# Four edits in the expert layer: x's scale and shift in 16 pieces, a sum's operand in PSUM, finer yields in the index work, fewer transposes on TensorE

## The chip, the cores and the metric

One core of one Trainium2 chip runs the whole kernel. The metric is the time of one execution in device microseconds (us), lower is better. The kernel before was run three times: 2249.8 us median, 2248.74 to 2251.46.

## What is computed

Two layers, each a mixer (two kinds of attention) and then an expert layer (`peer_ffn`), over 256 tokens of width 1024. All four edits lie in the expert layer:

```python
s1 = einsum('bshd,hnd->bshn', q[..., 0, :], sub_keys[0]);  s2 = ...      # 8 heads, 128 keys each
v1, i1 = top_k(s1, 16);  v2, i2 = top_k(s2, 16)
cand = (v1[..., :, None] + v2[..., None, :]).reshape(B, S, PEER_HEADS, 256)
cand_idx = (i1[..., :, None] * 128 + i2[..., None, :]).reshape(...)
top, pos = top_k(cand, 16)
idx = take_along_axis(cand_idx, pos, axis=-1)
gates = softmax(top, axis=-1)
act = gelu(einsum('btd,bthkd->bthk', hb, peer_u[ib]))
out = einsum('bthk,bthkd->btd', gb * act, peer_v[ib])
x = layer_norm(DN_ALPHA * x + out * gt2, ln_g[l, 1], ln_b[l, 1])
```

`layer_norm` ends in a scale by `ln_g` and a shift by `ln_b`. That of the mixer's norm is the one that the first edit cuts into pieces.

## The kernel before

The expert layer doesn't gather. It multiplies all 16384 experts with all tokens: 128 tiles j of `peer_u` (128 experts by 1024), in what is called the U stage here, then 128 tiles of `peer_v` (the V stage). The gates are a matrix of experts by tokens that is zero where an expert wasn't chosen. Every fp32 weight is split into a high half `wh` (ACT copies it to fp32r) and a low half `wl` (weight minus `wh`), and each product is three matmuls: hi x hi, lo x hi, hi x lo. A U tile is 24 matmuls with 256 columns, a V tile 12 with 512.

**Supply of a tile.** `take` hands out a tile that `prep` has split; `fetch` issues the DMA of a tile five ahead on SP's queue (5 buffers `raw`); `turn` transposes a `u` tile one or two ahead on DVE (`STREAM_TRANSPOSE`, L220, in blocks of 32x32, for which the DMA has arranged the rows). Of every four U tiles the fourth is of kind `x`: its DMA lays the rows out plainly, and `prep` (L246 to L251) transposes it on TensorE with eight 128x128 transposes into two PSUM banks, out of which ACT copies `wh` and then the weight itself (L263, L264). In the U stage POOL makes both `wl` of a tile (L271). In the V stage DVE makes them, with the low half of the gated activations (L521) before them.

**Side work.** While TensorE multiplies U tiles, the generators in `sides` make the gates. After each tile `pull` (L635) lets them go on until a credit is used up: 1.55 after a `u` tile, 2.75 after an `x` tile, and each `yield` gives the cost of what came before it. So the written order of DVE's instructions, its transposes among them, follows from these numbers. `select` is first `topk`: for 16 units (8 heads, 2 halves of the tokens) `key_ops` finds 16 best keys in each half, and zipped with it `cand_ops` of the unit before adds the candidates (L1400) and finds the best 16. TensorE's scores for a unit are issued one unit ahead (`scores`, L1371), and ACT copies them out of PSUM. Then the *index work* (L1443 to L1489) turns positions into expert numbers for each half of the tokens: small operations, then for either key a compare, a multiply and a reduce over 128x2048 (L1465, L1468, L1470). Then `place_gates`: 64 groups of 4 tokens, each two DVE operations, eight fp16 matmuls into a PSUM tile `G`, and their copies. The last two U tiles (126 and 127; `U_FIRST`) are multiplied after `sides` is drained.

**Scale and shift of x.** In the V stage, at j = 32, POOL issues the loads of `ln_g` and `ln_b` into rows of a free buffer, and at j = 38 and 44 multiplies and adds them to the two halves of x (L1726 to L1728).

## Time and profile before

| | before |
|---|---|
| runs | 2249.8 us median (2248.74 to 2251.46) |
| profiled execution | 2254.38 us, its span 2252.6 us |
| busy: PE, DVE, ACT, POOL | 95%, 81%, 52%, 46% |
| mean granted clock of TensorE | 0.982 |
| chain that ended last, by engine | PE 73%, DVE 16%, DMA 4%, ACT 3%, issue 3%, POOL 1% |
| chain, by line: U tiles, V tiles, transposes of `x` tiles | 28%, 27%, 2% |

How to read it: times are us from the span's start. The profiled execution is one run; its span is the time from its first to its last instruction. "Busy" is the time in which an engine had an instruction under way, waits inside it included. The chain of work is followed back from the last instruction, at each step to what released it. In the rows below an engine's idle time before an instruction stands in brackets, with what ended it.

### The profile page before, as it was taken

To read this page: it belongs to the slowest core of one execution; us is meant where nothing else is said; L and a number is where in the kernel's file an instruction comes from. 1 tells how busy PE (TensorE), PEld (TensorE's weight loads), DVE (VectorE), ACT (ScalarE), POOL (GpSimd) and SP (SyncE) were. 2 spreads that over 40 slices of the span, in tenths; PEclk is the share of its full clock that TensorE was granted. 3 is DMA by queue.
4 is the path that set the end of the run, shared out by engine and by line. 5 is a ranking of instruction groups with operands and counts; after the bars stand their busy time and mean duration, and the time that the engine had idled before them with its cause. 6 is when DMAs were issued, how large, how long until landed. Compare 5 with 4: busy or idle time off the path is not lost.

```text
span 2252.6 us, 42211 instructions
## 1 busy us (share of the span) xinstructions
PE 2135.2 (95%) x14596; PEld 1945.4 (86%) x14596; DVE 1817.2 (81%) x3278; ACT 1172.5 (52%) x2445; POOL 1041.5 (46%) x760
## 2 busy tenths in 40 slices
PE   5789899899999999999989998998999999999998
PEld 5789799899999978888779897997999999788886
DVE  7887989999997488888887558999999955666675
ACT  3446555455555545555545564554555555455562
POOL 4656637787778510000045534577777783200001
PEclk8999999999999999999999999999999999999999
DMA  8646567666667678888844335675766676666662
GB/s 273 196 137 221 159 140 159 129 148 148 142 147 156 176 236 275 281 286 283 298 134 150 113 121 142 147 153 118 154 142 148 146 164 187 202 196 192 193 227 90
DMA packets 498895, 400.32 MB, mean 178 GB/s; under 512 B 291920, under 2 KB 446072, under 8 KB 498680
## 3 DMA queue, kind: packets, MB, share of 16 engines
q1 hardware_dynamic: 496936, 392.33, 62.8%
q0 software_dynamic: 1408, 4.23, 0.6%
q8 instruction: 115, 1.88, 0.3%
q10 hardware_dynamic: 336, 1.06, 0.1%
q14 instruction: 100, 0.82, 0.1%
HBM read 396.46 MB, written 1.05 MB: 176 GB/s over the span
## 4 chain that ended last, share of the span: by engine, by line
PE 73%; DVE 16%; DMA 4%; issue 3%; ACT 3%; POOL 1%; SPq 1%; POOLq 0%; ACTq 0%; DVEq 0%
PE A L61 28%; PE Y L61 27%; PE T L61 7%; PE G L61 4%; PE T L251 2%; DVE wl L271 2%; PE ss L61 2%; PE hs L61 2%; DMA raw<-in_peer_u_dram 2%; POOL wl L271 1%; DVE qk L857 1%; DMA raw<-in_peer_v_dram 1%; DVE raw L220 1%; DVE e L843 1%; DVE o L1504 1%
## 5 line engine op out<-in xcount | busy, mean ns | idle before, releaser
L271 POOL TENSOR_TENSOR wl<-raw,wh 128x512 fp32r<-128x512 f32 x663 | 914.3, 1406 | 700.9 <-ACT wh L58 582.4
L58 ACT ACTIVATE wh<-raw 128x512 fp32r<-128x512 f32 x1060 | 610.8, 623 | 182.0 <-PE A L61 47.6
L61 PE MATMUL A<-hTh,wh 128*128 128x256 f32 x2080 | 543.3, 293 | 11.9 <-ACT wh L58 11.8
L61 PE MATMUL A<-hTl,wh 128*128 128x256 f32 x2080 | 524.2, 284 | 0.0
L61 PE MATMUL Y<-wh,o 128*128 128x512 f32 x1776 | 480.5, 392 | 0.8 <-DVE o L521 0.8
L271 DVE TENSOR_TENSOR wl<-raw,wh 128x512 fp32r<-128x512 f32 x525 | 380.2, 765 | 63.5 <-ACT wh L58 44.9
L61 PEld LDWEIGHTS A<-hTh,wh 128*128 128x128 f32 x2080 | 400.6, 193 | 14.4 <-ACT wh L58 13.7
L61 PEld LDWEIGHTS A<-hTl,wh 128*128 128x128 f32 x2080 | 401.7, 193 | 0.8 <-DVE hTl L521 0.2
L61 PEld LDWEIGHTS Y<-wh,o 128*128 128x128 f32 x1776 | 334.9, 189 | 70.8 <-DVE o L521 1.2
L61 PE MATMUL A<-hTh,wl 128*128 128x256 f32 x2080 | 337.9, 285 | 11.0 <-POOL wl L271 10.9
L61 PEld LDWEIGHTS A<-hTh,wl 128*128 128x128 f32 x2080 | 288.9, 193 | 14.2 <-POOL wl L271 14.2
L61 PE MATMUL Y<-wl,o 128*128 128x512 f32 x888 | 277.9, 393 | 10.4 <-DVE wl L271 10.4
L220 DVE STREAM_TRANSPOSE raw<-raw 128x1024 f32<-128x1024 f32 x192 | 235.1, 1230 | 11.7 <-DMA raw<-in_peer_u_dram 10.1
L58 ACT ACTIVATE o<-buf 128x256 fp32r<-128x256 f32 x228 | 95.1, 417 | 282.7 <-PE Y L61 282.7
L521 DVE TENSOR_TENSOR o<-buf,o 128x256 fp32r<-128x256 f32 x228 | 100.1, 439 | 150.4 <-ACT o L58 150.4
L61 PEld LDWEIGHTS Y<-wl,o 128*128 128x128 f32 x888 | 168.1, 189 | 48.9 <-DVE wl L271 13.8
L1499 DVE TENSOR_TENSOR o<-iT,iota_t 128x1024 f16<-128x1024 f16 x128 | 163.9, 1280 | 0.0
L58 ACT ACTIVATE buf<-G 128x128 f32<-128x128 f32 (+4 forms) x244 | 56.0, 276 | 203.6 <-PE G L61 203.6
L570 POOL TENSOR_TENSOR x<-x,buf 128x1024 f32<-128x1024 f32 x1 | 2.4, 2392 | 291.0 <-DVE x L567 291.0
L61 PE MATMUL T<-hTh,wh 128*128 128x256 f32 x512 | 133.6, 293 | 0.0
L61 PE MATMUL T<-hTl,wh 128*128 128x256 f32 x512 | 130.1, 286 | 0.0
L1504 DVE TENSOR_TENSOR o<-gT,o 128x1024 f16<-128x1024 f16 x128 | 124.6, 973 | 4.4
(496 smaller groups left out, 3254.9 us busy)
## 6 DMA issues: line engine op xcount, KB each, us to landing
raw<-in_peer_u_dram SPq DMA_DIRECT2D x1024, 128.0 KB, 3.5
raw<-in_peer_v_dram SPq DMA_DIRECT2D x256, 512.0 KB, 4.4
raw<-in_w_in_dram SPq DMA_DIRECT2D x88, 512.0 KB, 4.9
raw<-in_w_ada_dram SPq DMA_DIRECT2D x78, 512.0 KB, 4.9
raw<-in_w_o_dram SPq DMA_DIRECT2D x16, 512.0 KB, 3.5
raw<-in_w_pq_dram SPq DMA_DIRECT2D x64, 128.0 KB, 3.4
qk<-in_w_ada_dram SPq DMA_DIRECT2D x10, 512.0 KB, 3.9
e<-in_w_ada_dram SPq DMA_DIRECT2D x8, 512.0 KB, 6.0
```

The costliest lines, as they stand in the source:

```text
L58: nc.scalar.activation(o, i, f, **kw)
L61: nc.tensor.matmul(o, a, b, start=start, stop=stop, **kw)
L220: nc.vector.transpose(t, t)
L251: nc.tensor.transpose(banks[s][:, q], t[:, (4 * s + q) * P:(4 * s + q + 1) * P], ident)
L271: eng.tensor_sub(lo, src, h.bitcast(F32))
L521: nc.vector.tensor_sub(lo, src, h.bitcast(F32))
L570: nc.gpsimd.tensor_mul(xt[tt], xt[tt], last[0])
L843: eng.tensor_sub(ev[:, :, :hn], mid, bv[:, :, :hn])
L857: nc.vector.tensor_mul(tv[:, :, hn:], nodes(qT, n)[:, :, hn:], ev[:, :, hn:])
L1499: nc.vector.tensor_tensor(o.rearrange("p a u n v -> p (a u) n v"), iT[:, b].rearrange("p a (u v) -> p (a u) v", v=2)[:, :, None] .to_broad ...
L1504: nc.vector.tensor_mul(og.rearrange("p u a n v -> p (u a) n v"), gT[:, b * nu:(b + 1) * nu].rearrange("p u a v -> p (u a) v")[:, :, None] ...
```

## The change

Four edits, all but the first in `peer`:

1. `uv_seq`: tiles 103, 107, ..., 127 (seven in each layer) are of kind `u`, no longer `x`.
2. `topk`: a PSUM tile `vp` is added. Before the two candidate sums of a unit ACT copies the 16 values of the first key list into it (128x16), a yield of cost 0 follows, and both sums read that operand from PSUM.
3. Index work: yields after each of the first operations, and higher costs for the compare (1.4 to 1.7) and the reduce (1.4 to 1.6). What it charges in all goes from 0.9 + 7.8 to 4.2 + 8.8 for each half of the tokens.
4. x's scale and shift: 16 instructions on 256 columns, one after each of the V tiles 38 to 53, in place of four on 1024 columns.

```diff
-    uv_seq = [("x" if j % 4 == 3 else "u", j) for j in range(NK)] + [("v", j) for j in range(NK)]
+    uv_seq = [("x" if j % 4 == 3 and j < 100 else "u", j) for j in range(NK)] + [("v", j) for j in range(NK)]
@@ topk
+                    vp = psk.tile([P, 2, PH, TOPK], F32, name="G")
+
@@ cand_ops
                         at = 0
+                        act(vp[:, tt, h], v[0][tt][:, h], AF.Copy)
+                        yield 0.0
                         for a0, a1, w in segs:
                             dims = [P, a1 - a0, w]
                             nc.vector.tensor_add(cd[:, at:at + dims[1] * w].rearrange("p (a b) -> p a b", b=w),
-                                                 v[0][tt][:, h, a0:a1, None].to_broadcast(dims),
+                                                 vp[:, tt, h, a0:a1, None].to_broadcast(dims),
                                                  v[1][tt][:, h, None, :w].to_broadcast(dims))
@@ index work
                             nc.vector.tensor_scalar(sel[a].bitcast(U32), puf, 4 - 2 * a, None,
                                                     op0=OP.logical_shift_right)
+                            yield 0.5
                             nc.vector.tensor_copy(half[2 + a], iu[a][tt].rearrange("p h k -> p (h k)").bitcast(U32))
+                            yield 0.6
 
                         nc.vector.scalar_tensor_tensor(half[0], sel[1].bitcast(U32), -12.0, sel[0].bitcast(U32),
                                                        op0=OP.add, op1=OP.max)
+                        yield 0.5
                         for a in range(2):
                             nc.vector.scalar_tensor_tensor(sel[a], half[0], -16.0 + 12 * a, puf, op0=OP.mult, op1=OP.add)
+                            yield 0.5
                         nc.vector.scalar_tensor_tensor(half[1], sel[1], -48.0, sel[0], op0=OP.add, op1=OP.max)
                         tp = top[tt]
-                        yield 0.9
+                        yield 0.5
                         for a in range(2):
                             nc.vector.tensor_tensor(m, per_head(half[a])[:, :, :, None].to_broadcast(k4),
                                                     iota_k[:, None, None].to_broadcast(k4), op=OP.is_equal)
-                            yield 1.4
+                            yield 1.7
                             nc.vector.tensor_mul(m, m, per_head(half[2 + a])[:, :, None].to_broadcast(k4))
                             yield 1.1
                             nc.vector.tensor_reduce(per_head(sel[a]), m, axis=mybir.AxisListType.X, op=OP.add)
-                            yield 1.4
+                            yield 1.6
@@ V stage
-                    if j in (NB_J + 6, NB_J + 12):
-                        xb = from_blocks(xt[j // 6 - (NB_J + 6) // 6])
-                        nc.gpsimd.tensor_mul(xb, xb, in_blocks(g_row))
-                        nc.gpsimd.tensor_add(xb, xb, in_blocks(b_row))
+
+                    n = j - NB_J - 6
+                    if 0 <= n < 16:
+                        xb = from_blocks(xt[n // 8])[:, n % 4]
+                        (nc.gpsimd.tensor_add if n // 4 % 2 else nc.gpsimd.tensor_mul)(
+                            xb, xb, in_blocks(b_row if n // 4 % 2 else g_row)[:, n % 4])
```

How the instructions move. First DVE, where the index work of layer 0 begins; `buf` is the scratch memory of the side work, and each `STREAM_TRANSPOSE` is the transposing of one later `u` tile. The order before:

```order
L220 STREAM_TRANSPOSE raw<-raw 128x1024
L1444 COPY buf_3125<-buf_3125 128x8
L1445 TENSOR_TENSOR buf_3125<-buf_3125 128x128
L1444 COPY buf_3125<-buf_3125 128x8
L1445 TENSOR_TENSOR buf_3125<-buf_3125 128x128
L1453 TENSOR_SCALAR buf_3125<-buf_3125 128x128
L1455 CAST buf_3125<-buf_3125 128x128
L1453 TENSOR_SCALAR buf_3125<-buf_3125 128x128
L1455 CAST buf_3125<-buf_3125 128x128
L1457 SCALAR_TENSOR_TENSOR buf_3125<-buf_3125 128x128
L1460 SCALAR_TENSOR_TENSOR buf_3125<-buf_3125 128x128 x2
L1461 SCALAR_TENSOR_TENSOR buf_3125<-buf_3125 128x128
```

And of the change, from the same transpose (that of tile 28) on:

```order
L220 STREAM_TRANSPOSE raw<-raw 128x1024
L1448 COPY buf_3125<-buf_3125 128x8
L1449 TENSOR_TENSOR buf_3125<-buf_3125 128x128
L1448 COPY buf_3125<-buf_3125 128x8
L1449 TENSOR_TENSOR buf_3125<-buf_3125 128x128
L1457 TENSOR_SCALAR buf_3125<-buf_3125 128x128
L1460 CAST buf_3125<-buf_3125 128x128
L220 STREAM_TRANSPOSE raw<-raw 128x1024
L1457 TENSOR_SCALAR buf_3125<-buf_3125 128x128
L1460 CAST buf_3125<-buf_3125 128x128
L1463 SCALAR_TENSOR_TENSOR buf_3125<-buf_3125 128x128
L1467 SCALAR_TENSOR_TENSOR buf_3125<-buf_3125 128x128 x2
```

The next transpose has moved up by six small instructions. Over the whole of the index work the transposes of tiles 28 to 41, eleven, stand before or between its instructions in the order before; in that of the change those of tiles 28 to 45, fourteen.

Second ACT, in the top-k of layer 0: `buf<-K` is the copy of the scores of the unit that follows, `wh<-raw` and `wh<-T` the splitting of weight tiles, `G<-buf` the new copy.

```order
 L58 ACTIVATE buf_3123<-A 128x512
 L58 ACTIVATE buf_3125<-K 128x256
+L58 ACTIVATE G<-buf_3125 128x16
 L58 ACTIVATE wh<-raw 128x4x4x32 x2
 L58 ACTIVATE buf_3125<-K 128x256
+L58 ACTIVATE G<-buf_3125 128x16
 L58 ACTIVATE wh<-raw 128x4x4x32 x2
 L58 ACTIVATE buf_3123<-A 128x512
 L58 ACTIVATE wh<-raw 128x4x4x32 x2
 L58 ACTIVATE buf_3125<-K 128x256
+L58 ACTIVATE G<-buf_3125 128x16
 L58 ACTIVATE wh<-T 128x512
```

The new copy stands behind the copy of the scores of the next unit, or behind the splits of the tile after.

Third POOL, in the V stage of layer 0, with the loads of the two rows in front.

```order
 L434 DMA buf_3123<-in_ln_g_dram 128x1024
 L434 DMA buf_3123<-in_ln_b_dram 128x1024
-L1727 TENSOR_TENSOR x_79<-x_79,buf_3123 128x4x8x32
-L1728 TENSOR_TENSOR x_79<-x_79,buf_3123 128x4x8x32
-L1727 TENSOR_TENSOR x_80<-x_80,buf_3123 128x4x8x32
-L1728 TENSOR_TENSOR x_80<-x_80,buf_3123 128x4x8x32
+L1737 TENSOR_TENSOR x_79<-x_79,buf_3123 128x8x32 x8
+L1737 TENSOR_TENSOR x_80<-x_80,buf_3123 128x8x32 x8
```

Nothing else of POOL stands between the pieces. They wait for the two loads and for one another, and for no other engine.

## Rows read from the trace of the kernel before

**Rows 1.** Timeline of PE: start, us, engine, instruction; transposes of six `x` tiles.

```profile
409.13 1.03 PE L251 MATMUL T<-ident,raw 128*128 128x128 f32 x8
474.68 1.04 PE L251 MATMUL T<-ident,raw 128*128 128x128 f32 x8
...
757.79 1.04 PE L251 MATMUL T<-ident,raw 128*128 128x128 f32 x8
770.18 1.04 PE L251 MATMUL T<-ident,raw 128*128 128x128 f32 x8
...
1512.57 1.04 PE L251 MATMUL T<-ident,raw 128*128 128x128 f32 x8
1581.03 1.04 PE L251 MATMUL T<-ident,raw 128*128 128x128 f32 x8
```

**Rows 2.** Busy time by stretches: PE, PEld, DVE, ACT, POOL, granted clock, DMA share, GB/s.

```profile
420.00:430.00 10.00, 7.64 (x47) 6.81 (x45) 9.93 (x7) 3.03 (x4) 5.45 (x3) 0.83 0.31 85
660.00:670.00 10.00, 9.98 (x96) 9.69 (x95) 9.93 (x15) 5.32 (x16) 7.82 (x6) 1.00 0.62 139
740.00:750.00 10.00, 10.00 (x87) 10.00 (x86) 3.24 (x4) 5.42 (x11) 7.71 (x8) 1.00 0.86 191
```

**Rows 3.** Timeline of DVE in the index work of layer 0.

```profile
415.10 1.25 DVE L220 STREAM_TRANSPOSE raw<-raw 128x1024 f32<-128x1024 f32 x1
...
426.51 2.29 DVE L1470 TENSOR_REDUCE buf<-buf 128x128 f32<-128x2048 f16 x1
...
469.45 1.23 DVE L220 STREAM_TRANSPOSE raw<-raw 128x1024 f32<-128x1024 f32 x1
```

**Rows 4.** Instructions of line 1400: duration in ns, shortest/median/longest; first and last start.

```profile
L1400 DVE TENSOR_TENSOR buf<-buf x64: 178/310/1366, 324.0 to 1516.3; 128x64 f32<-128x64 f32 x32, 128x48 f32<-128x48 f32 x32
```

**Rows 5.** Timelines of POOL and DVE in the last norm of the kernel.

```profile
2240.75 2.45 POOL L571 TENSOR_TENSOR x<-x,buf 128x1024 f32<-128x1024 f32 x1
...
2241.34 0.67 DVE L531 TENSOR_TENSOR buf<-Y,buf 128x512 f32<-128x512 f32 x1
```

**Rows 6.** Groups of instructions: count | busy us, mean ns | idle before, releaser.

```profile
L1400 DVE TENSOR_TENSOR buf<-buf 128x64 f32<-128x64 f32 x64 | 40.6, 637 | 0.0
...
L58 ACT ACTIVATE buf<-K 128x256 f32<-128x256 f32 (+1 forms) x34 | 13.5, 396 | 60.3 <-PE K L61 60.2
```

**Rows 7.** Timeline of POOL: splits late in the U stage, x's scale and shift (layer 0).

```profile
722.56 10.08 POOL L271 TENSOR_TENSOR wl<-raw,wh 128x512 fp32r<-128x512 f32 x8 [2.29 <-ACT raw L58]
...
834.82 2.37 POOL L1728 TENSOR_TENSOR x<-x,buf 128x1024 f32<-128x1024 f32 x1 [3.55 <-DMA buf<-in_ln_b_dram]
837.15 2.58 POOL L1727 TENSOR_TENSOR x<-x,buf 128x1024 f32<-128x1024 f32 x1
839.80 2.67 POOL L1728 TENSOR_TENSOR x<-x,buf 128x1024 f32<-128x1024 f32 x1
```

**Rows 8.** Timeline of DVE at the same place.

```profile
834.84 2.64 DVE L521 TENSOR_TENSOR o<-buf,o 128x256 fp32r<-128x256 f32 x1 [0.27 <-ACT o L58]
837.40 5.62 DVE L271 TENSOR_TENSOR wl<-raw,wh 128x512 fp32r<-128x512 f32 x2
```

**Rows 9.** Timeline of ACT in the V stages: the copy that begins each V tile.

```profile
825.99 0.42 ACT L58 ACTIVATE o<-buf 128x256 fp32r<-128x256 f32 x1 [0.26 <-PE Y L61]
...
849.32 0.42 ACT L58 ACTIVATE o<-buf 128x256 fp32r<-128x256 f32 x1 [1.49 <-PE Y L61]
...
1929.52 0.42 ACT L58 ACTIVATE o<-buf 128x256 fp32r<-128x256 f32 x1 [1.26 <-PE Y L61]
1932.24 0.42 ACT L58 ACTIVATE o<-buf 128x256 fp32r<-128x256 f32 x1 [1.26 <-PE Y L61]
...
1954.13 0.42 ACT L58 ACTIVATE o<-buf 128x256 fp32r<-128x256 f32 x1 [2.48 <-PE Y L61]
```

**Rows 10.** Busy time by stretches, the steady V stage of either layer.

```profile
1000.00:1100.00 100.00, 100.00 (x448) 81.78 (x447) 82.45 (x137) 55.01 (x113) 0.00 (x0) 1.00 0.86 285
2000.00:2100.00 100.00, 100.00 (x443) 82.81 (x442) 63.01 (x111) 54.17 (x111) 0.00 (x0) 1.00 0.61 193
```

## Prediction, made before the changed kernel was run

> **What bounds the kernel now.** I read the page first: TensorE (PE) is busy 95% of the span and carries 73% of the chain that ended last. So a microsecond is won only where PE waits, runs at its lower clock, or does work that can go. The timeline of PE shows both places in the U stage, because one `x` tile in every four is marked by its transposes. Late in the stage, with no side work left, two marks lie 12.39 us apart [rows 1]: 96 products and eight transposes, with PE never idle (10.00 of 10 in that stretch, rows 2). Between 409.13 and 474.68 there are four such spacings of four tiles, 65.55 us where 4 x 12.39 = 49.6 would do [rows 1]. In layer 1 it is 1512.57 to 1581.03, 68.46 us. About 0.8 us of each is PE's own work there (six more transposes at 1.04 / 8). So the index work costs PE 15.2 and 18.1 us, **33.3 us in all**. The stretches show how: in 420 to 430 PE is busy 7.64 of 10 at a mean granted clock of 0.83, while DVE is busy 9.93 [rows 2]. A clock of 0.83 is a third of the time at 1.2 GHz and the rest at 2.4, after PE had stood idle. DVE's order says why: from the transpose of tile 28 at 415.10 to that of tile 42 at 469.45 [rows 3] DVE takes 54.35 us to give PE 14 tiles, which PE could do in 14 x 12.39 / 4 = 43.4.
>
> The second loss is in the V stage. A V tile begins with a copy on ACT, 2.72 us after the last one (1929.52 to 1932.24, rows 9). Around x's scale and shift five tiles take 23.33 us in layer 0 (825.99 to 849.32) and 21.89 in layer 1 (1932.24 to 1954.13), where 5 x 2.72 = 13.6 would do [rows 9]: **9.7 and 8.3 us lost, 18.0 in all**. There two splits on DVE take 5.62 us under POOL's operations, and one small one 2.64 [rows 7, 8].
>
> **Candidate sums from PSUM.** Removed: 64 sums of 637 ns, 40.6 us of DVE [rows 6], 20.3 a layer. Their shortest is 178 ns, their longest 1366 [rows 4]; the long ones are waits for a POOL split, of which one takes 10.08 / 8 = 1.26 us [rows 7]. No sum of 64 columns with a PSUM operand is in the trace. The nearest row is a product of 512 columns from PSUM: 0.67 us, wholly inside a POOL operation of 2.45 us [rows 5], so not held up by it. That bounds the new sum by 0.18 below and 0.67 above; I take 0.2, since it has an eighth of the columns. DVE saves 20.3 - 32 x 0.2 = 14 us a layer (bounds 14.5 and -1). This lies under PE, which isn't idle in the top-k, so by itself it is worth nothing there. What it gives is lead: DVE enters the index work with its transposes further ahead. Now PE would begin tile 28 at 409.13 + 0.9 + two tiles of 2.9, about 415.8, and its transpose begins at 415.10 [rows 1, 3]; a transpose alone is 1.25 us and a split on ACT and one on POOL follow, so PE is late from the first index instruction on.
>
> The price is a wait. Each unit's sums now wait for ACT, whose copy stands behind the copy of the next unit's scores, and that one waits for PE: 60.3 us over 34 copies [rows 6]. So DVE can no longer run more than about a tile ahead of PE in the top-k. Behind a waiting sum on DVE stand the unit's other operations and the next transposes. I estimate that it costs PE 1 us a layer, and that it caps the spare lead at tile 28 at about 2 us. ACT itself has room (5.4 of 10 busy, rows 2); 64 short copies, at most 0.4 us each by the nearest row (rows 6, 256 columns), lie in its idle time.
>
> **Index work by instruction.** It removes and adds no work; it moves transposes forward. The new order has 18 tiles between the transposes of 28 and of 46, where it had 14. PE needs 18 x 12.39 / 4 = 55.8 us for them. DVE needs its 54.35 us and three transposes more, 3 x 1.2, so 58 us. That is nearly even, where it was short by 11. The costs still charge too little (a reduce of 2.29 us [rows 3] is charged 1.6, before 1.4), so DVE falls behind within the stretch: laid end to end between the new transposes, most at tile 42, by about 5 us. With 2 us of spare lead that leaves 3 us of stall, with the 1 us above **4 us a layer**, where 15.2 and 18.1 were lost. Bounds: 0, if the lead covers all, and 9, if there is no lead and POOL holds DVE up more often. The two edits together: 33.3 - 8 = **25.3 us gained** (15 to 33).
>
> The gate groups begin four tiles later and end at about tile 113, still before 126, so no work is pushed past the U stage: there DVE is busy only 3.24 of 10 [rows 2] and has room for it.
>
> **Transposes up to tile 100.** Seven tiles a layer lose their eight transposes on PE. By count they are 8 / 104 of the 12.39 us, 0.95; the row says 1.04, end overlapping the next product [rows 1]. I take 0.9: 2 x 7 x 0.9 = 12.6 us, all on the path, since PE is never idle there. Each tile also spares ACT two copies and gives DVE a transpose of 1.23 us. From about tile 113 on DVE has the room [rows 2]. Tiles 103, 107 and 111 still fall into the gates, where DVE is busy 9.93 of 10 [rows 2]: 3 x 1.23 = 3.7 us of DVE there, of which the thinner gates (ten groups over fourteen tiles, after the smaller credit) cover most; I take 0.6 a layer as lost. POOL's two splits, 2.5 us, still fit into a tile of 2.9. **Gain 11.4 us** (bounds 5 and 14).
>
> The Trainium skill speaks against this edit: VectorE: DVE Perf Modes, Rules for kernel authors, advises TensorE for a 128x128 transpose if PSUM will do as its destination, and DVE for blocks of 32x32. By it the seven tiles should stay, and the edit would gain nothing. The row that decides here is PE's own, busy 10.00 of 10 [rows 2], with DVE at 3.24.
>
> **x's scale and shift in pieces.** POOL has 16 pieces for four operations. A 1024-column operation takes 2.37 us, one of 512 takes 1.26 [rows 7]; so 0.15 fixed, and a piece of 256 about 0.7: 11.3 us a layer, for 10.0. The pieces stand in the program a tile apart, but nothing holds POOL back: twelve of them will run one after another when the second row has landed, at 834.82 now. What changes is how DVE gets in. Now three POOL operations let three DVE instructions through, one each [rows 7, 8]. If that stays so, 16 pieces delay 16 DVE instructions by 0.7 us, spread over some five tiles. Per tile DVE is busy 0.63 x 2.72 = 1.7 us in layer 1 and 0.82 x 2.72 = 2.2 in layer 0 [rows 10], so has 1.0 and 0.5 us to give. Layer 1: 11.3 - 5 x 1.0 - 2 for the slack of a split that PE needs only late in its tile, 4 us lost, for 8.3. Layer 0: 11.3 - 4.5 x 0.5 - 2, 7 lost, for 9.7. **Gain 7 us** (bounds -3, if all of POOL's time is lost as now and 1.3 us a layer more, and 18).
>
> By the Trainium skill (SBUF — State Buffer, Who interferes with whom) the port that DVE and POOL share is locked for a whole instruction and the loser is blocked, not slowed; shorter instructions then alter the turns and not the sum. The rows agree with the lock; by the sum alone this edit would gain nothing, which is the first rival.
>
> **Sum.** 25.3 + 11.4 + 7 = 43.7 us. The profiled execution of 2254.4 us would be 2210.7; it stands 4.6 above the median of 2249.8, so the median comes to **2206 us**.
>
> **The rivals.**
> - *The lock's time is conserved.* PE loses the 18 us of the V stage as before. For it: POOL's pieces run in a burst and are 1.3 us longer a layer. Against: DVE's idle time per tile. 2206 + 7 to 10 = 2214 to 2216.
> - *DVE stays late.* The lead is used up by the wait for ACT, and half of the index loss stays: 33.3 / 2 = 16.6 in place of 25.3 gained, 2215. For it: DVE's need of 58 us over PE's 55.8.
> - *The moved transposes pay nothing,* because POOL or DVE takes PE's place as the bound from tile 100: 2206 + 11.4 = 2217. Against: POOL at 7.71, DVE at 3.24 of 10 [rows 2].
> - *Slower: the copy through ACT ties DVE to PE.* In each of 32 units DVE sits out the wait of ACT's score copy, 60.3 / 34 = 1.8 us, and the copies after it, 0.4: 70 us, of which the 28 us saved on sums pay a part. 42 us come out on PE as late transposes, and no lead is left, so that half of the index gain goes (12 us): 2206 + 42 + 12 = 2260. It decides where the wait eats DVE's spare time of about 1 us a unit. Against: that copy waits mostly because PE is behind DVE, which doesn't hurt PE.
>
> **How the numbers follow.** Chances: forecast 0.58, conserved lock 0.18, DVE late 0.11, transposes 0.07, slower 0.06. Two rivals at once give 2224 to 2226; all edits at their best ends 2250 - 33 - 14 - 12 = 2191. The range **2192 to 2226** holds the first four cases, nine in ten less a little for bad sizes. A measurement here tells 0.2%, 4.5 us, from no change. The slower case at half its price falls inside that: faster 0.94, same 0.02, slower 0.04.
>
> **What would show it.** Right: marks of `x` tiles about 13 us apart all through the index work; PE's clock back at 1.00 there; candidate sums of about 0.2 us without long ones; late U tiles 2.9 us each; POOL's pieces of 0.7 us back to back, DVE's splits under them at about 1.4. Wrong: DVE idle before the candidate sums for more than 1 us a unit with PE waiting behind it, PE waiting for POOL's `wl` after tile 100, or V tiles that still lose 8 us a layer.

## The result, and the profile after

The changed kernel takes **2228.19 us** (median of four runs, 2226.93 to 2228.48), the kernel before 2250.12 beside it (2248.74 to 2251.46): ratio 0.99 [0.9884, 0.9915], **21.9 us faster**. The forecast was 2206, range 2192 to 2226. The direction was right, the gain half of the forecast, and the time lies 2 us outside the range. The profiled execution took 2227.97 us, 26.4 less than that of before, which stood some 4 us over its median; the terms below account for 25.5 of these 26.4.

The page of the changed kernel, its busy times and its chain by engine:

```profile
PE 2117.0 (95%) x14484; PEld 1928.0 (87%) x14484; DVE 1819.4 (82%) x3296; ACT 1164.5 (52%) x2443; POOL 1063.8 (48%) x784
...
PE 69%; DVE 15%; DMA 5%; issue 3%; ACT 3%; POOL 2%; SPq 1%; POOLq 0%; ACTq 0%; DVEq 0%
```

POOL's share of the chain has gone from 1% to 2%, and DVE's 16% has hardly fallen. The marks say where. From the timeline of PE of the changed kernel, for each layer: the transposes of tiles 27, 47 and 99, and the first product of the V stage.

```profile
408.47 1.04 PE L251 MATMUL T<-ident,raw 128*128 128x128 f32 x8
...
481.10 1.04 PE L251 MATMUL T<-ident,raw 128*128 128x128 f32 x8
...
672.14 1.04 PE L251 MATMUL T<-ident,raw 128*128 128x128 f32 x8
...
769.34 1.09 PE L61 MATMUL Y<-wh,o 128*128 128x512 f32 x4
...
1502.16 1.04 PE L251 MATMUL T<-ident,raw 128*128 128x128 f32 x8
...
1574.81 1.04 PE L251 MATMUL T<-ident,raw 128*128 128x128 f32 x8
...
1765.06 1.04 PE L251 MATMUL T<-ident,raw 128*128 128x128 f32 x8
...
1862.24 1.09 PE L61 MATMUL Y<-wh,o 128*128 128x512 f32 x4
```

In the order of the prediction:

- **Index work.** It now spans five spacings of four tiles, 408.47 to 481.10 and 1502.16 to 1574.81: 72.63 and 72.65 us. Five times 12.39 [rows 1] and PE's own 0.8 are 62.75, so 9.9 us a layer are lost, where it was 15.2 and 18.1. Gained: 13.5 us, not 25.3.
- **Late U stage.** From the mark of tile 99 to the first V product: 97.20 and 97.18 us. Before it was 97.17 and 97.06, with seven `x` tiles' transposes in it (6.1 us) but four gate groups fewer (four tiles with gates take 14.6 us, without 12.39, so 2.2). On balance 3.9 us a layer should have gone, and nothing went. The U stage outside the index work gained 3.8 us over both layers, not 11.4; that is the 2.2 a layer which the gate groups left behind in its middle, less small change.
- **Scale and shift.** V tiles around it lose 7.1 us in layer 0 and 2.7 in layer 1, where it was 9.7 and 8.3. Gained: 8.2 us, forecast 7.

13.5 + 3.8 + 8.2 = 25.5 of the 26.4.

Busy time by stretches, changed kernel (PE, PEld, DVE, ACT, POOL, granted clock, DMA share, GB/s):

```profile
420.00:430.00 10.00, 7.80 (x62) 7.16 (x61) 9.97 (x9) 4.74 (x9) 7.63 (x5) 1.00 0.44 106
430.00:440.00 10.00, 8.45 (x69) 8.04 (x69) 9.90 (x8) 3.12 (x6) 10.00 (x7) 1.00 0.73 155
...
720.00:730.00 10.00, 8.69 (x78) 8.49 (x77) 9.23 (x14) 4.90 (x10) 8.55 (x7) 1.00 0.49 128
...
740.00:750.00 10.00, 10.00 (x85) 10.00 (x85) 5.74 (x6) 5.40 (x9) 9.66 (x9) 1.00 0.80 212
```

Against [rows 2]: in 420 to 430 the granted clock is back at 1.00 (2.4 GHz), and still PE is busy 7.80 of 10 only. DVE is as full as before, and POOL has gone from 5.45 of 10 to between 7.63 and 10.00. In 720 to 730, about tile 112, PE now idles with DVE at 9.23; after 740 it is full.

The candidate sums, all instructions of the line (duration in ns, shortest/median/longest), and what DVE waited for ahead of them (us, times):

```profile
L1404 DVE TENSOR_TENSOR buf<-G,buf x64: 170/208/226, 323.6 to 1503.6; 128x64 f32<-128x64 f32 x32, 128x48 f32<-128x48 f32 x32
...
  ACT G L58: 20.8, 16
```

The 0.2 us is as forecast, and the long ones of [rows 4] are gone: the longest fell from 1366 to 226 ns. DVE waits 20.8 us for ACT's copy over both layers, but PE doesn't show it: most `x` marks in the top-k stand 13.2 us apart, as before.

Timeline of DVE in the index work of layer 0, changed kernel, from the transpose of tile 28 to that of tile 46:

```profile
411.77 1.25 DVE L220 STREAM_TRANSPOSE raw<-raw 128x1024 f32<-128x1024 f32 x1
...
414.24 0.22 DVE L1457 TENSOR_SCALAR buf<-buf 128x128 uint32<-128x128 uint32 x1
414.38 0.22 DVE L1460 CAST buf<-buf 128x128 f16<-128x128 uint32 x1
...
415.67 0.99 DVE L1457 TENSOR_SCALAR buf<-buf 128x128 uint32<-128x128 uint32 x1
416.58 1.33 DVE L1460 CAST buf<-buf 128x128 f16<-128x128 uint32 x1
417.83 1.41 DVE L1463 SCALAR_TENSOR_TENSOR buf<-buf 128x128 f16<-128x128 uint32 x1
...
424.31 2.17 DVE L1476 TENSOR_TENSOR buf<-buf 128x2048 f16<-128x2048 f16 x1
...
474.98 1.23 DVE L220 STREAM_TRANSPOSE raw<-raw 128x1024 f32<-128x1024 f32 x1
```

DVE took 63.2 us for this stretch, forecast 58. Many operations on 128 columns take 1.0 to 1.4 us here. The same shift and cast take 0.22 where no split of POOL is under way (at 414.24 and 414.38, ahead of the next transpose).

The other side of it is POOL. What PE's weight loads (PEld) waited for between the marks of tiles 27 and 47 in layer 0 (us, times, longest), and one row of POOL's timeline there:

```profile
PEld A L61 <- POOL wl L271: 8.4, 9, 1.7
PEld A L61 <- ACT wh L58: 0.6, 2, 0.4
...
422.77 17.88 POOL L271 TENSOR_TENSOR wl<-raw,wh 128x512 fp32r<-128x512 f32 x10 [2.37 <-ACT wh L58]
```

So most of the 9.9 us appears on PE as waits for a `wl` of POOL. The row has ten splits in 17.88 us, 1.79 each, where most splits take 1.30. Eight splits of this stretch take 2.26 to 3.31 us, each of them beside a compare or a multiply of DVE, and eight of the nine waits (8.1 us) end when one of these eight ends. The two engines hold each other up: DVE's instructions get longer, and so do POOL's, by 10.3 us a layer.

### The profile page after: what moved, and what is told of

Its sections match the earlier page's. It is cut to its first block, busy times and chain, and to the rows that moved or that the text cites. A ratio compares the mean times of both kernels' runs of the same rounds, so it can differ in the third digit from the quotient of the medians.

```text
span 2226.2 us, 42039 instructions
## 1 busy us (share of the span) xinstructions
PE 2117.0 (95%) x14484; PEld 1928.0 (87%) x14484; DVE 1819.4 (82%) x3296; ACT 1164.5 (52%) x2443; POOL 1063.8 (48%) x784
## 4 chain that ended last, share of the span: by engine, by line
PE 69%; DVE 15%; DMA 5%; issue 3%; ACT 3%; POOL 2%; SPq 1%; POOLq 0%; ACTq 0%; DVEq 0%
PE Y L61 27%; PE A L61 25%; PE T L61 7%; PE G L61 3%; DMA raw<-in_peer_u_dram 3%; POOL wl L271 2%; PE hs L61 2%; DVE wl L271 2%; PE ss L61 2%; PE T L251 2%; DMA raw<-in_peer_v_dram 1%; DVE qk L857 1%; DVE o L1512 1%; SPq L197 1%; DVE e L843 1%
## 5 line engine op out<-in xcount | busy, mean ns | idle before, releaser
L271 POOL TENSOR_TENSOR wl<-raw,wh 128x512 fp32r<-128x512 f32 x663 | 925.7, 1421 | 662.0 <-ACT wh L58 587.3
L58 ACT ACTIVATE wh<-raw 128x512 fp32r<-128x512 f32 x1088 | 627.7, 622 | 206.8 <-PE A L61 59.0
L61 PE MATMUL A<-hTh,wl 128*128 128x256 f32 x2080 | 336.2, 284 | 13.5 <-POOL wl L271 13.4
L220 DVE STREAM_TRANSPOSE raw<-raw 128x1024 f32<-128x1024 f32 x206 | 252.8, 1233 | 3.2 <-DMA raw<-in_peer_u_dram 2.7
L58 ACT ACTIVATE buf<-G 128x128 f32<-128x128 f32 (+6 forms) x236 | 53.8, 273 | 202.7 <-PE G L61 202.7
L1512 DVE TENSOR_TENSOR o<-gT,o 128x1024 f16<-128x1024 f16 x128 | 131.3, 1025 | 4.4
```

What stands on the lines that cost most here:

```text
L58: nc.scalar.activation(o, i, f, **kw)
L61: nc.tensor.matmul(o, a, b, start=start, stop=stop, **kw)
L220: nc.vector.transpose(t, t)
L271: eng.tensor_sub(lo, src, h.bitcast(F32))
L1512: nc.vector.tensor_mul(og.rearrange("p u a n v -> p (u a) n v"), gT[:, b * nu:(b + 1) * nu].rearrange("p u a v -> p (u a) v")[:, :, None] ...
```

## The experiments

Each ratio is to the kernel before, run beside it on the same chip. A difference to the changed kernel, as "20.7 us below", sets medians of separate rounds side by side; the median of the kernel before lay between 2250.1 and 2252.5 in them, so a difference of two or three microseconds alone shows nothing. First each edit alone, on the kernel before.

**Yields alone** (edit 3):

```diff
                                                     op0=OP.logical_shift_right)
+                            yield 0.5
...
-                            yield 1.4
+                            yield 1.7
...
-                            yield 1.4
+                            yield 1.6
```

> The kernel before with the finer yields of the index work alone. Theory (lock): DVE's index instructions with two SBUF inputs each wait out a POOL split once PE runs and POOL is busy, so the stretch costs DVE some 63 us and not the 58 of the prediction; and DVE enters it without lead. PE then loses about 12 us a layer where it lost 15 to 18: 7 to 11 us faster than before, 2239 to 2243. Rival (the prediction's own account, DVE needs 58 us): PE loses 5 to 7 a layer, 20 us or more faster, 2230 or less.

Measured 2241.67 us (2238.58 to 2244.24), ratio 0.9952 [0.9936, 0.9969]. The five spacings come to 74.89 and 75.38 us, a loss of 12.1 and 12.6.

**PSUM operand alone** (edit 2):

```diff
+                        act(vp[:, tt, h], v[0][tt][:, h], AF.Copy)
+                        yield 0.0
...
-                                                 v[0][tt][:, h, a0:a1, None].to_broadcast(dims),
+                                                 vp[:, tt, h, a0:a1, None].to_broadcast(dims),
```

> The kernel before with the candidate sums from PSUM alone. Theory: the sums shrink to 0.2 us, which gives DVE a lead of about 3 us at the index work where it had 0.6, so PE loses 2 to 3 us a layer less: 4 to 6 us faster, 2244 to 2246. Rival (the new wait of DVE for ACT's copy makes transposes late in the top-k): no faster or slower, 2250 to 2255, with spacings of the x tiles above 13.3 us in the top-k. Rival (the whole index loss came from the sums): 15 us or more faster.

2246.99 us (2244.37 to 2250.29), 0.9983 [0.9973, 0.9992]. With the old yields the four spacings are 63.36 and 65.43, each 2 to 3 us better. So the lead it gives is worth 2 to 3 us a layer with either set of yields.

**Fewer transposes alone** (edit 1):

```diff
-("x" if j % 4 == 3 else "u", j)
+("x" if j % 4 == 3 and j < 100 else "u", j)
```

> The kernel before with the transposes of tiles 103 to 127 moved to DVE alone. In this kernel the gate groups end at tile 107 or 108. Theory (what ate the gain was DVE, saturated by gate groups that now reach to tile 113): five of seven tiles a layer fall behind the gates and gain 0.87 us each, the other two gain nothing: 7 to 9 us faster, 2241 to 2243. Rival (POOL's splits or the DMA bound a stretch of u tiles alone): no faster, 2248 to 2252, with late u tiles at 3.1 us where 2.9 would do.

2242.77 us (2241.79 to 2247.64), 0.9956 [0.994, 0.9973]. Here the stretch from tile 99 to the V stage falls to 91.92 and 92.21 us, 5 less. With the old yields only six of a layer's 64 gate groups come after tile 99, where the changed kernel has ten, and more of the moved transposes fall behind them.

**Pieces alone** (edit 4 of the list, the one that cuts up the scale and shift of the mixer's norm):

```diff
-                    if j in (NB_J + 6, NB_J + 12):
...
+                    n = j - NB_J - 6
+                    if 0 <= n < 16:
...
```

with one instruction on 256 columns at each. 

> The kernel before with x's scale and shift in 16 pieces alone. Theory (one DVE instruction gets in between two POOL instructions, and DVE has idle time per tile to give, more in layer 1): the loss at this place falls from 8.3 to about 2.7 us in layer 1 and from 9.7 to about 8 in layer 0: 6 to 8 us faster, 2242 to 2244. Rival (the lock's time is conserved): 2249 to 2253.

2244.58 us (2240.05 to 2248.54), 0.9968 [0.9955, 0.998].

The four gains are 9.6, 4.3, 8.5 and 6.7, in sum 29.1 us; together they give 21.9. Some 7 us are given back between the edits. The intervals of five medians are about as wide as that, but the marks show 6.3 us of it after tile 99: alone, edit 1 shortens the stretch to the V stage by 5.3 and 4.9 us, and behind the new yields only from 99.1 (yields alone) to 97.2 in both layers. Edit 3 pushes gate groups to where edit 1 loads DVE.

**Is the index work charged too little?** The costs of the yields set to what the operations take:

```diff
-                            yield 0.5
+                            yield 0.9
...
-                            yield 1.7
+                            yield 2.3
...
-                            yield 1.1
+                            yield 2.2
...
-                            yield 1.6
+                            yield 2.3
```

> The changed kernel with the index work charged near what it takes: small operations 0.9, compare 2.3, multiply 2.2, reduce 2.3. Its instructions then spread over five tiles more, and the gate groups end at about tile 124. Theory (DVE's need in the index work is 63 us in 18 tiles where PE needs 56): the index loss falls from 10 to about 2 us a layer, and part of it comes back after tile 100, where more gate groups meet the transposes, some 2 to 4 us a layer: 8 to 12 us faster than the changed kernel, 2216 to 2220. Rival (all of the U stage is bound by DVE, so the loss only moves): within 3 us, 2225 to 2231.

2226.19 us (2225.52 to 2227.43), 0.9889 [0.9873, 0.9906]. The rival holds, the loss moved: the seven spacings from tile 27 to 55 (93.39 us) lose only 5.9 us, but from tile 99 to the V stage it is 106.48 us, 9.3 more. So the costs only place the loss; from tile 28 to the end of the gates there is not enough time for the side work beside the tiles, wherever it is spent.

**Is it the lead that the copy caps?** ACT's copy moved to the end of the unit's first top-k, ahead of the next unit's score copy:

```diff
@@ key_ops, end
+                        act(vp[:, tt, h], v[0][tt][:, h], AF.Copy)
@@ cand_ops
-                        act(vp[:, tt, h], v[0][tt][:, h], AF.Copy)
-                        yield 0.0
```

> The changed kernel with ACT's copy into PSUM issued as soon as a unit's first key list is complete, ahead of the copy of the scores of the unit after next. Theory (that wait caps DVE's lead at about 3 us when the index work begins): DVE's idle time before candidate sums, 20.8 us in 16 waits, goes, the lead grows by 2 to 3 us, and PE loses that much less a layer: 3 to 6 us faster, 2222 to 2225. Rival (the cap on the lead comes from elsewhere, the buffers of tiles or the scores, or the stall recurs at every half of the index work): within 2 us of the changed kernel.

2223.59 us (2221.08 to 2223.9), 0.9879 [0.9863, 0.9896]. The spacings of the index work are 12.39, 17.39, 12.71, 16.27, 13.17 where the changed kernel has 13.07, 17.43, 12.71, 16.26, 13.16. Only the first is mended, 0.7 us a layer; the two long stalls stay. DVE's wait for the copy, which was expected to go, stays as well: 18.7 us in 8 waits, where it was 20.8 in 16. So the time falls into the range of the theory, but 1.4 us of the 4.6 are all that has a place in the index work. The lead was a small part.

**Is it DVE's transposes?** On top of the full charges, five more `x` tiles where the index work is:

```diff
-("x" if j % 4 == 3 and j < 100 else "u", j)
+("x" if j % 4 == 3 and j < 100 or j % 4 == 1 and 28 <= j < 48 else "u", j)
```

> full_charge with five more U tiles of kind x in either layer (29, 33, 37, 41, 45), so that DVE is spared five transposes of 1.23 us (6.2 us) and PE gets 5 x 0.87 = 4.4 us of work. Theory (DVE is the bound of the U stage from tile 28 on to about tile 118): the U stage gets shorter by 3 to 6 us a layer against full_charge, 2214 to 2220. Rival (PE is the bound over most of it, DVE only late by moments): PE's added work shows, 2228 to 2235.

2227.98 us (2225.47 to 2231.18), 0.9888 [0.9864, 0.9912]. By the marks neither comes true: from the mark of tile 27 to the first V product it takes 361.37 and 359.95 us, against 359.78 and 359.96 with the full charges. DVE's 6.2 us and PE's 4.4 a layer about cancel. Trading transposes between the two engines is no way out here.

**Is it POOL?** No splits on POOL for the tiles of the index work:

```diff
-            eng.tensor_sub(lo, src, h.bitcast(F32))
+            if kind in "ux" and 27 <= state.get("uj", 0) % NK < 48:
+                ls[-1] = hs[-1]
+            else:
+                eng.tensor_sub(lo, src, h.bitcast(F32))
...
```

> The changed kernel without POOL's splits for the U tiles 27 to 47 of either layer: their low half is not made, and the high half is multiplied in its place (so these tiles count twice; the products are as many as before). DVE's order is untouched. Theory (POOL's splits hold up DVE's small index operations): those that took 0.9 to 1.5 us fall to 0.2 to 0.5, DVE needs 50 to 53 us from the transpose of tile 28 to that of tile 46 in place of 63.2, the five spacings after the mark of tile 27 come to 62 to 65 us in place of 72.6, and the time to 2208 to 2216. Rival (DVE's own work is what is too long): the five spacings stay above 69 and the time at 2221 or more.

2207.44 us (2206.28 to 2209.62), 0.9799 [0.9776, 0.9822]: 20.7 us below the changed kernel. The five spacings are 63.03 and 63.02 us, PE's own time to 0.3 us. The DVE timeline of this kernel shows the same operations as above, in the same order (lines are 5 further down):

```profile
411.60 1.25 DVE L220 STREAM_TRANSPOSE raw<-raw 128x1024 f32<-128x1024 f32 x1
...
415.10 0.19 DVE L1462 TENSOR_SCALAR buf<-buf 128x128 uint32<-128x128 uint32 x1
415.20 0.22 DVE L1465 CAST buf<-buf 128x128 f16<-128x128 uint32 x1
415.34 0.28 DVE L1468 SCALAR_TENSOR_TENSOR buf<-buf 128x128 f16<-128x128 uint32 x1
...
419.71 1.23 DVE L1481 TENSOR_TENSOR buf<-buf 128x2048 f16<-128x2048 f16 x1
...
463.56 1.24 DVE L220 STREAM_TRANSPOSE raw<-raw 128x1024 f32<-128x1024 f32 x1
```

0.99 us has become 0.19, 1.33 is 0.22, 1.41 is 0.28, the multiply 1.23 for 2.17. The transposes (1.23 to 1.25) are as before, and so are the reduces (2.24 in both). The whole stretch takes DVE 52.0 us, with some of it now waiting for PE, instead of 63.2. This run takes away both sides of the hold-up at once: DVE's own operations get shorter, as the rows show, and the splits for which PE's weight loads waited 8.4 us are not there at all. It shows that the loss comes from running the two side by side, and not which side PE feels.

Three windows over this stretch, of the kernel before, the changed one and this one:

```profile
415.00:469.40 54.40, 45.19 (x334) 42.94 (x334) 52.40 (x58) 24.17 (x44) 42.11 (x27) 0.94 0.57 123
```

```profile
411.70:474.90 63.20, 56.43 (x453) 54.16 (x452) 62.26 (x61) 31.04 (x57) 55.06 (x37) 1.00 0.68 143
```

```profile
411.50:463.50 52.00, 52.00 (x439) 52.00 (x439) 46.10 (x61) 30.82 (x55) 0.00 (x0) 1.00 0.96 178
```

Without POOL, DVE's 61 instructions are 46.10 us of work. In the changed kernel they took 62.26, so 37 splits held DVE up for 16.2 us, 0.44 each on average. In the kernel before there are three transposes fewer, 46.10 - 3 x 1.24 = 42.4, and it took 52.40: 10.0 us over 27 splits, 0.37 each.

**Do operands in PSUM take the hold-up away?** Four intermediates of the index work into the bank of `vp`, as f32:

```diff
-                    vp = psk.tile([P, 2, PH, TOPK], F32, name="G")
+                    vs = psk.tile([P, 4, P], F32, name="G")
+                    vp = vs[:, :2].rearrange("p t (h k) -> p t h k", h=PH)
...
-                    half = [carve(n // 2).bitcast(F16) for _ in range(4)]
+                    es = [vs[:, 2], sel[1]]
+                    half = [vs[:, 3], vs[:, 2], vs[:, 0], vs[:, 1]]
```

and `es` for `sel` in the operations up to L1469. 

> The changed kernel with four of the index work's 128x128 intermediates in PSUM as f32 (one of the two shifted lists, and the four half lists), so that of its small operations before the compares all but the second shift have an operand or their result there. The computation is the same. Theory (what POOL's splits hold up are operations whose operands all lie in SBUF): those with a PSUM operand take 0.2 to 0.5 us under a busy POOL in place of 1.3 to 1.5, some 4 to 5 us of DVE a layer; the five spacings after the mark of tile 27 come to 67.5 to 69.5 us in place of 72.6, the time to 2217 to 2222. Rival (the hold-up only moves to the next operation, or the multiply loses by its f32 PSUM operand what the others win): spacings above 71, the time 2225 or more.

**2214.84 us** (2212.44 to 2215.81), 0.9843 [0.9826, 0.9859]: 13.4 us below the changed kernel. The five spacings are 66.34 and 66.32 us, better than the theory's 67.5. DVE timeline of this kernel, same stretch:

```profile
412.92 1.25 DVE L220 STREAM_TRANSPOSE raw<-raw 128x1024 f32<-128x1024 f32 x1
...
417.08 0.73 DVE L1459 TENSOR_SCALAR buf<-buf 128x128 uint32<-128x128 uint32 x1
417.73 0.28 DVE L1462 CAST G<-buf 128x128 f32<-128x128 uint32 x1
418.05 0.30 DVE L1465 SCALAR_TENSOR_TENSOR G<-buf,G 128x128 f32<-128x128 uint32 x1
...
422.72 2.29 DVE L1478 TENSOR_TENSOR buf<-buf,G 128x2048 f16<-128x2048 f16 x1
...
470.84 1.23 DVE L220 STREAM_TRANSPOSE raw<-raw 128x1024 f32<-128x1024 f32 x1
```

Of the operations before the compares, what has an operand or its result in PSUM (`G`) takes 0.3 us; the one left wholly in SBUF (L1459, second list) still takes 0.73, and 0.80 for the other half of the tokens. The multiply loses its fast form (2.29, against 1.23 without POOL), which costs DVE next to nothing, since under POOL it took 2.17 anyway. DVE needs 57.9 us for the stretch. The window over it, and what PE's weight loads waited for:

```profile
412.90:470.80 57.90, 56.19 (x462) 54.88 (x461) 57.04 (x61) 31.85 (x57) 44.78 (x37) 1.00 0.76 156
...
PEld A L61 <- POOL wl L271: 1.1, 3, 0.4
```

DVE's 61 instructions fell from 62.26 to 57.04 us, and POOL's 37 splits from 55.06 to 44.78: with an operand of each compare and multiply in PSUM, no split of the stretch takes more than 1.36 us, and the wait for them falls from 8.4 to 1.1. The theory spoke only of DVE's small operations; what it left out, POOL's splits beside the long ones, changed by twice as much. No run moves the one without the other, so how the 13.4 us divide between them stays open.

**Why do the moved transposes pay nothing?** First, PE transposes up to tile 115:

```diff
-("x" if j % 4 == 3 and j < 100 else "u", j)
+("x" if j % 4 == 3 and j < 116 else "u", j)
```

> The changed kernel with tiles 103, 107, 111 and 115 back on TensorE, so that only 119, 123 and 127 are moved. Theory (between tiles 100 and 114 DVE is the bound, by gate groups and transposes): giving PE back four sets of transposes costs nothing, since DVE is spared 1.23 us for each 0.87 on PE: within 2 us of the changed kernel, 2226 to 2229. Rival (PE is the bound there, as the prediction had it): 8 x 0.87 = 7 us slower than the changed kernel, 2235.

2224.93 us (2224.36 to 2228.69), 0.989 [0.9874, 0.9907]. From tile 99 to the V stage: 96.50 and 96.50 us. Four tiles' transposes are back on PE (3.5 us), and the stretch isn't longer: what PE does more, it had waited before. Then without POOL's splits for tiles 100 to 117 of the changed kernel:

```diff
+            if kind in "ux" and 100 <= state.get("uj", 0) % NK < 118:
+                ls[-1] = hs[-1]
...
```

> The changed kernel without POOL's splits for the U tiles 100 to 117 of either layer: their low half is not made, and the high half is multiplied in its place. DVE's order is untouched. Theory (the moved transposes fall where DVE, held up by POOL's splits, is the bound of the gates' tail): from the mark of tile 99 to the first V product 93.4 to 95 us a layer in place of 97.2, the time 2220 to 2224. Rival (DVE's own work, or the order of the gate groups, binds there, with POOL or without it): 96.5 us or more, the time 2226 or more.

2218.58 us (2216.21 to 2220.2), 0.9862 [0.9845, 0.9878]. The stretch falls from 97.2 to 92.99 us in both layers, a little more than expected. A window of this kernel, to set beside that of the changed one:

```profile
720.00:730.00 10.00, 10.00 (x86) 10.00 (x85) 7.65 (x10) 5.91 (x11) 0.00 (x0) 1.00 0.69 196
```

PE is full where it was at 8.69. In the changed kernel PE had waited, from 672 to 770 us, as follows (us, times, longest):

```profile
PE G L61 <- DVE o L1512: 3.0, 3, 1.3
PE A L61 <- POOL wl L271: 0.2, 1, 0.2
```

L1512 is the second DVE operation of a gate group: its mean after tile 99 is 1.22 us, and 0.69 without the splits. So the 3.9 us that the moved transposes should have given are lost where POOL holds DVE up; here, other than in the index work, it is DVE that PE waits for.

**What do the pieces of x still cost?** In the changed kernel POOL runs them as soon as the rows have landed. Timeline of POOL, the pieces in either layer:

```profile
821.96 2.77 POOL L1737 TENSOR_TENSOR x<-x,buf 128x256 f32<-128x256 f32 x4
827.31 13.23 POOL L1737 TENSOR_TENSOR x<-x,buf 128x256 f32<-128x256 f32 x12 [2.57 <-DMA buf<-in_ln_b_dram]
...
1913.15 2.81 POOL L1737 TENSOR_TENSOR x<-x,buf 128x256 f32<-128x256 f32 x4
1918.08 11.82 POOL L1737 TENSOR_TENSOR x<-x,buf 128x256 f32<-128x256 f32 x12 [2.12 <-DMA buf<-in_ln_b_dram]
```

and DVE's splits at the same places:

```profile
821.02 4.26 DVE L271 TENSOR_TENSOR wl<-raw,wh 128x512 fp32r<-128x512 f32 x2
...
1912.40 4.12 DVE L271 TENSOR_TENSOR wl<-raw,wh 128x512 fp32r<-128x512 f32 x2
...
1919.72 2.37 DVE L271 TENSOR_TENSOR wl<-raw,wh 128x512 fp32r<-128x512 f32 x2
```

The first four pieces ran in 2.8 us, and DVE's pair of splits beside them took 4.1 to 4.3 us instead of 1.3: all of the 2.8. Later pairs took 2.37. To hold each piece to its V tile, a copy of one column that depends on that tile's activations was put ahead of it on POOL:

```diff
+                        nc.gpsimd.tensor_copy(pace, wsplit[-1][1][:, :1].bitcast(F32))
```

> The changed kernel with a copy of one column before each piece on POOL that reads the low half of the next tile's activations, so that each piece waits for DVE's progress and one piece falls on a tile. Theory (twelve pieces in a burst are more than DVE's idle time there can take): spread over 16 tiles they cost nothing in layer 1 and 1 to 4 us in layer 0, where they now cost 2.7 and 8: 5 to 9 us faster than the changed kernel, 2219 to 2223. Rival (the lock's time comes out on PE however it is spread): within 2 us.

2220.72 us (2219.57 to 2224.31), 0.9871 [0.9854, 0.9887], 7.5 below the changed kernel. Timeline of POOL in layer 1 of this kernel:

```profile
1961.45 0.18 POOL L1738 COPY pace<-o 128x1 f32<-128x1 f32 x1 [53.63 <-DVE o L522]
1961.59 1.18 POOL L1739 TENSOR_TENSOR x<-x,buf 128x256 f32<-128x256 f32 x1
1964.23 0.70 POOL L1738 COPY pace<-o 128x1 f32<-128x1 f32 x1 [1.46 <-DVE o L522]
1964.89 1.20 POOL L1739 TENSOR_TENSOR x<-x,buf 128x256 f32<-128x256 f32 x1
```

The pieces now run some 50 us later, at the tiles beside which they are written, one in each tile, and V tiles of layer 1 lose nothing. In layer 0 some 1.6 us stay, most of it one late weight tile (ACT waits 2.64 us for it), nearly 50 us ahead of the first piece.

**Together.** The changed kernel with the paced pieces, the early copy and `x` tiles up to 115. 

> The changed kernel with paced, early_copy and x_to_116 at once. Alone they came to 7.5, 4.6 and 3.3 us below the changed kernel. If the three gains lie in different places (V stage, top-k, the gates' tail): 2211 to 2216. If those of early_copy and x_to_116 are the same microseconds of DVE, or mere scatter: 2217 to 2221.

2219.44 us (2217.09 to 2220.16), 0.985 [0.9827, 0.9874]: little better than the pacing alone. The marks do show gains in both U stages: from the mark of tile 27 to the first V product 358.77 and 358.54 us, where the paced kernel has 360.98 and 360.14. But from there to the mark of tile 27 in layer 1 this profiled execution takes 731.4 us, the paced one 727.7; why is not known, and the next kernel has 727.2 again. With the PSUM operands of the index work on top: 

> all_three with the PSUM operands of index_psum. If the index work's stall is shortened as said for index_psum and the rest stays: 2209 to 2215. If index_psum gains nothing: 2217 to 2222.

**2205.61 us** (2203.49 to 2208.42), 0.9808 [0.9791, 0.9825], the fastest kernel here that computes everything: 44.6 us below before and 22.6 below the change. That is better than expected. Its five index spacings come to 65.63 and 65.64 us.

## Why the prediction was half right

- **What bounds the kernel: right.** The two places named first gave 21.7 of the 25.5 us. The clock in the index work went back to 1.00 as expected; the marks, which should have stood about 13 us apart there, stood 12.7 to 17.4 apart.
- **Candidate sums: right in size** (0.2 us). The 1 us a layer charged for the wait on ACT did not show in the top-k; the cap on the lead did, with 0.7 us (early copy).
- **Index work: the step that failed** is "DVE needs its 54.35 us and three transposes more, 3 x 1.2, so 58 us." DVE took 63.2 us. The step carried 54.35 us over as if it were DVE's own work. 10.0 us of it was hold-up by 27 splits of POOL, and POOL makes two splits for every tile that PE gets. Four more tiles in the stretch bring more splits (ten by the windows, eight by the count of tiles): 10 x 0.37 = 3.7 us, so 61.7; that each one cost 0.44 in the end adds 2.4, and DVE stood idle 1.1 us less. A repair that speeds PE up brings its own obstacle with it. And the step has no term for the other side: PE's own wait for the splits, which DVE's compares and multiplies held up, 8.4 us a layer, is at nothing in it. In front of the prediction lay what was needed: it put the long candidate sums [rows 4] down to waits for a split, and didn't apply this to the operations of the next stage. The upper bound of that term, 9 us a layer "if there is no lead and POOL holds DVE up more often", is nearly what came (9.9).
- **POOL's hold on DVE was priced for the candidate sums and the V stage only,** and stood in the index work as a bound alone. There, operations on 128 columns wholly in SBUF took 1.0 to 1.4 us beside a split and 0.2 to 0.3 without POOL, reduces 2.24 and transposes 1.23 in both, and operations with an operand in PSUM 0.3. The Trainium skill, SBUF — State Buffer, Who interferes with whom, has just these classes: a DVE operation with two SBUF inputs contends with a GpSimd (POOL) operation that reads SBUF, and one in a two-port mode, as a copy, a cast or an operation with a scalar can be, contends with GpSimd; one with at most one SBUF input outside these modes does not, and a reduce never does. The rows agree with these classes; no row shows the mode of an operation. The prediction weighed that section for the V stage and left the index work out.
- **Transposes: the step that failed** is "I take 0.6 a layer as lost." Lost were 3.9. The thinner gates did not cover DVE's extra work, again beside a busy POOL: it was at 8.5 of 10 there, and without its splits the stretch came to 92.99. Alone the edit was worth 8.5 us, so its worth depends on edit 3, which moves the gates' end behind it.
- **Pieces: right in sum** (8.2 for 7), wrong in the turns: four pieces passed without any turn for DVE between them, the later ones with one. And that POOL runs ahead of the text was seen, but not that holding it back was worth as much again.
- **From the profile to the median: 4.6 us of the 22 missed.** The sum took its terms from an execution 4.6 us above the median and then took 4.6 us off the forecast, as if the changed kernel's profiled execution would stand as far above its own. It stands at the median (2227.97 and 2228.19).
- **The rivals.** "DVE stays late" and "the moved transposes pay nothing" both came true in what they cost; the text gave 2224 to 2226 for two at once. The reason given for the first, a lead used up by the wait for ACT, did not: that was 0.7 us a layer. The text treated them as separate cases of 0.11 and 0.07, though both hang on one cause, DVE beside a busy POOL. With that seen, the case of both together belonged in the middle of the range.
- **The low end.** 2191 for "all edits at their best" takes 12 us for the pieces, where their own bound is 18; by the bounds it is 2185. The miss lies at the other end.

Open: how much of the index work's loss is DVE's lateness with the transposes, which lets POOL begin late, and how much the lengthening of POOL's splits, at whose ends PE waits. Leaving the splits out removes both at once, and so do the operands in PSUM.

## What to carry to other kernels

A stage's busy time on DVE beside a busy POOL is not its work: measure it where POOL is idle, and price an edit that raises the rate of tiles with the POOL work that comes with each tile. The same holds the other way: look at the length of POOL's instructions beside DVE's long ones with two inputs (here 2.26 to 3.31 us in place of 1.30), and at which of the two the engine behind them waits for. Where DVE can't get away from POOL, put one operand of its operations, the long ones too, into a spare PSUM bank; here 1.0 to 1.4 us became 0.3, the splits went back to 1.30, and the kernel was 13 us faster. And an engine with no data to wait for runs its side work at once, in a burst; if it should be spread over the tiles, it needs a dependency on them.

## What the runs showed that was not expected

Four back-to-back POOL pieces of 0.7 us passed while a DVE split waited through all of them (4.26 us for two splits), so shorter POOL instructions did not by themselves give DVE turns. Two edits with gains of 9.6 and 8.5 us alone overlapped by most of the 7 us that the four together fell short of their sum. And a multiply that lost its fast form through a PSUM operand (1.23 to 2.29 us) cost next to nothing, since beside POOL the fast form took 2.17; POOL's splits beside it and the compare became shorter by more than a microsecond each on average.
